# The last twelve convolved tiles woven into the first attention units in a fixed TensorE order, and the slow modulation columns summed once, with none beside top-k

## The chip, the cores and the metric

The kernel runs on one core of one Trainium2 chip. The core has five engines that run their own instruction queues: TensorE (PE; its weight loads are shown apart as PEld), VectorE (DVE), ScalarE (ACT), GpSimd (POOL) and SyncE (SP), which starts the transfers. The metric is the device time of one execution in microseconds, taken as the median of several runs. A profile is one further execution with the hardware profiler on, and its trace gives start and length of every instruction.

## The reference, cut to what matters

One layer of a streaming encoder, for one sequence of 1024 positions with 1024 features, all in float32. It has a mixer sub-layer and a feed-forward sub-layer, both between norms and both modulated by a vector c.

```python
mod = silu(c) @ ada_w + ada_b             # 6 x 1024 values: shift, scale and gate of two sub-layers
h = rmsnorm(x) * (1 + scale) + shift
proj = h @ w_in                           # one projection for everything below
q_lat, kv_lat, k_idx, w_idx, z, xbc, dt, gate_a, gate_b = split(proj)

# A: sparse attention, per block of 128 queries
score = sum_heads(w_idx * relu(q_idx @ k_idx.T))        # only keys of admissible chunks
idx = top_k(score, 256)
logits = q @ kv[idx].T * scale + bias(position)
att = softmax(logits) @ kv[idx] @ w_uv                  # 16 heads, 64 values each

# B: state-space mixer
xbc = silu(causal_depthwise_conv(xbc, width 4) + conv_b)   # 4096 channels
y = ssd(xbc, dt) ; y = rmsnorm(y * silu(z))

out = x + gate * norm((sigmoid(gate_a) * (att @ w_o1) + sigmoid(gate_b) * (y @ w_o2)) @ w_out)
out = out + gate2 * norm(swiglu(modulated norm of out))
```

## The kernel before, in words

Everything is kept transposed: features on the 128 partitions, positions along the free axis in two halves of 512. Each float32 operand of a large product is split into a high part and a low part, and a product is three matmuls (high by high, low by high, high by low). For weights, ScalarE rounds the high part (whi, L151) and GpSimd subtracts it to get the low part (wlo, L152). Raw weight pieces come in 256 KB transfers into four buffers, the high and low parts have three buffers each, so the splits run only a little ahead of TensorE.

The stages in order are: norm and the first 16 columns of the modulation; latents; the scores of the indexer; keys and values; **top-k**, which runs on VectorE and ScalarE as a search with counts and ends in `mark` (L693 to L702) on VectorE, which writes the masks MK; the **attention units**; the rest of the state-space mixer; the merge; the feed-forward layer.

Beside top-k and attention, the kernel runs the **wide column tiles** of the input projection. A wide tile is 128 output features by 1024 positions: 48 matmuls of 128x512 (named pw) into two PSUM banks. There are 56: 32 convolved tiles (`conv`: one ScalarE pass, then three VectorE multiply-adds L904 to L906 that read the PSUM bank, then a silu), 16 z tiles (silu) and 8 a tiles (sigmoid), the latter two through `gate`. The string FILL gives their order: five groups of four convolved tiles, 16 z, 8 a, and three more groups.

An attention unit is one pair of heads (hp, 0 to 7) and one block of 256 queries (u, in U_ORDER 0, 2, 1, 3). `att_scores` makes the queries (puq, 12 matmuls; split into qh on ScalarE and ql on VectorE), adds the bias and the mask on GpSimd (nm, L750), makes the logits (plg), takes their maximum on VectorE while adding nm (L775), and the exponential on ScalarE (L778). `att_out` transposes the probabilities on TensorE (pt, L799), copies them (pc, L802 and L804, by turns on VectorE and ScalarE), multiplies with the values (po, L815) and scales the result (rb). `weave` takes steps of the scores of one unit and the output of the unit before in turn. It can take a third sequence z as well.

The **slow modulation columns** are the 32 of 48 that are needed late. `ada_slow` loads a 128x1024 block in two halves (adaw, two buffers), multiplies each by silu(c) on GpSimd (L316), sums each on VectorE (L317) and adds the two sums on GpSimd (L318). `ada_col` takes the sum over partitions with one TensorE product (adap, L285) and adds the bias on VectorE (mod, L286). `ada_next` starts one column and ends the one three before it.

What sets the order: the program is traced in Python, a scheduler then orders the instructions of each engine by a simulated time, with the traced order as priority. Inside `in_order(engines)` the named engines keep the traced order. Before the change the first 12 attention units (the first three pairs of heads, HP_FIRST) are traced ahead of FILL and their order is left to the scheduler, which puts wide tiles between them; ATT_ORDER is empty, so the later 20 units are left to it as well. PSUM banks come from two pools: `bank_d` has three banks (pw, adap, and pt from the fourth pair of heads on), `bank` five.

Of the kernel before, what the change touches and what calls it, by code (L numbers as in the profile page):

```python
# [17 lines left out]
P = 128  # L18
# [12 lines left out]
LOWEST = -BIGGEST  # L31
QC = 256
ORDERED = (mybir.EngineType.PE, mybir.EngineType.Activation, mybir.EngineType.DVE)
FILL = "xxxxx" + "z" * 16 + "a" * 8 + "xxx"
ADA_FROM = 21
HP_FIRST = 3
LEAD = 1.5
U_ORDER = (0, 2, 1, 3)
ATT_ORDER = ()
NCH = L // QC  # L40
PRODUCT = {n: i for i, n in enumerate("1567342")}
EARLY = 16
# [25 lines left out]
def build(tc, a, dbg=None, stop=99, slots=None):  # L68
# [26 lines left out]
    def half(b):  # L95
        return slice(512 * b, 512 * b + 512)
# [5 lines left out]
    def dump(key, ap, idx=None):  # L102
        if dbg is not None and key in dbg:
            d = dbg[key] if idx is None else dbg[key][idx]
            SP.dma_start(d, ap)
# [203 lines left out]

    def ada_slow(j):  # L310

        acc = EV("adas", (P, 2, P))
        for h in range(2):
            t = wp.tile([P, 4, P], F32, name="adaw", tag="adaw", bufs=2)
            behind(SP.dma_start(t, a["ada_w"][j - 16][:, 4 * h:4 * h + 4]))
            behind(G.tensor_tensor(t, t, cs[:, 4 * h:4 * h + 4, None].to_broadcast([P, 4, P]), op=OP.mult))  # L316
            V.tensor_reduce(acc[:, h], t.rearrange("p k m -> p m k"), axis=AX.X, op=OP.add)  # L317
        G.tensor_tensor(acc[:, 0], acc[:, 0], acc[:, 1], op=OP.add)  # L318
        return j, acc[:, 0]

    AHEAD = 4
    X0 = [[None, None] for _ in range(KT)]
# [522 lines left out]

    att = {}

    def attention(steps, last, beside=lambda: None):

        for s_ in steps + [None] * last:  # L850
            nxt = iter(())
            if s_ is not None:
                hp, u = s_
                if u == U_ORDER[0]:
                    vt = vp.tile([P, NT, P], F32, name="vt", bufs=1)
                    SP.dma_start(vt, d_v[hp])
                    att["w"] = small_weights(a["w_uq"][hp]), vt, load_bias(hp)
                uq, vt, nb = att["w"]
                PR = {}
                nxt = att_scores(u, uq, nb, PR)  # L860
            prev = att.get("prev")
            if prev is None:
                weave(nxt, 5, iter(()), 0)
            else:
                weave(nxt, 5 if s_ else 0, att_out(*prev), 2 * prev[1] + 3, lead=LEAD)
            if s_ is not None:
                att["prev"] = (hp, u, vt, PR)
            beside()

    if stop != 3:  # L870
        attention([(hp, u) for hp in range(HP_FIRST) for u in U_ORDER], 0)
        if stop == 4:
            attention([(hp, u) for hp in range(HP_FIRST, 8) for u in U_ORDER], 1)
    if stop == 4:
        for k in range(KT):
            for b in BS:
                t = EV("attd")
                SP.dma_start(t, d_att[k][:, half(b)])
                dump("attn", t, (k, slice(None), half(b)))
        ctx.close()  # L880
        return


    def wide(c):
        W.plan(col_tile(a["w_in"][c]))
        p = [bank_d("pw") for b in BS]
        dense([(p[b], b, ALL) for b in BS], wpieces(ks8), Hs)
        return p
# [6 lines left out]
            SP.dma_start(dst[:, half(b)], t)  # L895

    def conv(ch, dst):
        p = wide(17 + ch)
        ts = [EV("cv") for b in BS]
        for b in BS:  # L900
            S.activation(ts[b], p[b], AF.Identity, bias=col("conv_b", ch), scale=col("cw3", ch))  # L901
        for s, nm_ in ((1, "cw2"), (2, "cw1"), (3, "cw0")):
            w = col(nm_, ch)
            V.scalar_tensor_tensor(ts[0][:, s:], p[0][:, :512 - s], w, ts[0][:, s:], op0=OP.mult, op1=OP.add)  # L904
            V.scalar_tensor_tensor(ts[1][:, :s], p[0][:, 512 - s:], w, ts[1][:, :s], op0=OP.mult, op1=OP.add)
            V.scalar_tensor_tensor(ts[1][:, s:], p[1][:, :512 - s], w, ts[1][:, s:], op0=OP.mult, op1=OP.add)  # L906
        for b in BS:
            S.activation(ts[b], ts[b], AF.Silu)
            SP.dma_start(dst[:, half(b)], ts[b])
# [8 lines left out]
        if j is not None:  # L918
            late.append(ada_slow(j))

    def conv_group(g, ada):
        for ch, dst in ((16 + g, d_bc[g, 0]), (24 + g, d_bc[g, 1]), (2 * g, d_xs[2 * g]), (2 * g + 1, d_xs[2 * g + 1])):
            conv(ch, dst)
            if ada:
                ada_next()

    n_x, n_z, n_a = iter(range(GROUPS)), iter(range(16)), iter(range(8))
    for i, kind in enumerate(FILL):
        if kind == "x":
            conv_group(next(n_x), i >= ADA_FROM)  # L930
        elif kind == "z":
            t = next(n_z)
            gate(1 + t, d_z[t], AF.Silu)
        elif stop != 3:
            t = next(n_a)
            gate(49 + t, d_sga[t], AF.Sigmoid)
        if kind != "x" and i >= ADA_FROM:
            ada_next()
    if stop != 3:
        with in_order(*ATT_ORDER):  # L940
            attention([(hp, u) for hp in range(HP_FIRST, 8) for u in U_ORDER], 1, ada_next)
    for _ in range(35):
        ada_next()

# [700 lines left out]
```

## Time and profile before

| | us |
|---|---|
| median of 3 runs (lowest, highest) | 2447.46 (2446.3, 2448.2) |
| the profiled execution, its own time | 2449.83 |
| its span, first to last instruction | 2448.1 |
| mean granted TensorE clock | 0.985 |

Of the profile, a row of a timeline has the start and the length in microseconds, the engine, the line, the operation, the tiles out and in, and in brackets the engine's idle time before it with what ended it. A row of the waits has the engine and line that waited, the engine and line waited for, and the total, the number and the longest of the waits. A row of a group has its count, busy time, mean length in nanoseconds, and the idle time ahead. The windows have busy times of the engines in a stretch of time. Names of buffers are those of the program.

### The profile page before, as it was taken

To read this page: it belongs to the slowest core of one execution; us is meant where nothing else is said; L and a number is where in the kernel's file an instruction comes from. 1 tells how busy PE (TensorE), PEld (TensorE's weight loads), DVE (VectorE), ACT (ScalarE), POOL (GpSimd) and SP (SyncE) were. 2 spreads that over 40 slices of the span, in tenths; PEclk is the share of its full clock that TensorE was granted. 3 is DMA by queue.
4 is the path that set the end of the run, shared out by engine and by line. 5 is a ranking of instruction groups with operands and counts; after the bars stand their busy time and mean duration, and the time that the engine had idled before them with its cause. 6 is when DMAs were issued, how large, how long until landed. Compare 5 with 4: busy or idle time off the path is not lost. (4 is left out here: it accounts for less than half of the span.)

```text
span 2448.1 us, 35113 instructions
## 1 busy us (share of the span) xinstructions
PE 2360.6 (96%) x11878; PEld 1915.1 (78%) x11878; DVE 1598.2 (65%) x3109; ACT 1242.6 (51%) x2350; POOL 1052.2 (43%) x854
## 2 busy tenths in 40 slices
PE   7999999999899999999999999999899999999997
PEld 5888888887677787777776777887777888888877
DVE  4466775699765567866457677255466787556776
ACT  3456665577456665555656655353444222335452
POOL 1422112222443334622345445656577555544565
PEclk9999999999999999999999999999999999999999
DMA  7123222523322323311578885465375555328765
GB/s 269 61 88 122 67 70 81 152 93 106 115 90 86 97 93 120 106 40 61 190 226 266 284 261 195 161 213 164 99 241 168 168 191 178 117 95 299 229 212 168
DMA packets 227652, 369.85 MB, mean 151 GB/s; under 512 B 22624, under 2 KB 84752, under 8 KB 227472
## 3 DMA queue, kind: packets, MB, share of 16 engines
q1 hardware_dynamic: 226752, 367.03, 45.9%
q8 instruction: 94, 1.54, 0.3%
q14 instruction: 86, 0.70, 0.1%
q10 hardware_dynamic: 720, 0.58, 0.1%
HBM read 275.74 MB, written 94.92 MB: 151 GB/s over the span
## 5 line engine op out<-in xcount | busy, mean ns | idle before, releaser
L152 POOL TENSOR_TENSOR wlo<-wraw,whi 128x512 fp32r<-128x512 f32 x242 | 330.3, 1367 | 597.7 <-ACT whi L151 536.8
L1254 PE MATMUL p<-xh,wr 128*128 128x512 f32 x880 | 276.2, 392 | 5.8 <-DVE g L1304 4.2
L151 ACT ACTIVATE whi<-wraw 128x512 fp32r<-128x512 f32 x242 | 151.3, 627 | 229.6 <-issue 71.5
L1248 POOL TENSOR_TENSOR wr<-a,wr 128x512 fp32r<-128x512 f32 x110 | 155.6, 1422 | 124.3 <-ACT wr L1247 100.2
L1254 PEld LDWEIGHTS p<-xh,wr 128*128 128x128 f32 x880 | 166.4, 189 | 41.7 <-DVE g L1304 4.6
L1254 PE MATMUL p<-xl,wr 128*128 128x512 f32 x440 | 172.1, 391 | 0.0
L778 ACT ACTIVATE lg<-lg,mx 128x256 f32<-128x256 f32 (+7 forms) x128 | 98.4, 770 | 94.3 <-DVE mx L775 92.2
L1247 ACT ACTIVATE wr<-a 128x512 fp32r<-128x512 f32 x110 | 68.7, 629 | 145.4 <-PE p L1254 118.3
L1254 PE MATMUL p<-h2h,wr 128*128 128x512 f32 x352 | 111.9, 394 | 0.0
L638 ACT ACTIVATE junk<-acc,cand__2182 128x1024 bf16<-128x1024 f32 (+2 forms) x96 | 86.2, 898 | 46.4 <-DVE cand__2182 L681 28.6
L1426 PE MATMUL pfo<-ah,wlo 128*128 128x512 f32 x264 | 103.2, 391 | 2.1 <-POOL wlo L246 2.1
L1426 PE MATMUL pfo<-ah,whi 128*128 128x512 f32 x264 | 103.1, 390 | 0.4 <-ACT whi L245 0.4
L589 DVE SCALAR_TENSOR_TENSOR acc<-rel,widx,acc 128x384 f32<-128x384 f32 (+2 forms) x90 | 87.0, 986 | 24.9 <-ACT rel L584 24.7
L225 PE MATMUL pos<-yh,whi 128*128 128x512 f32 x256 | 100.8, 395 | 2.5 <-ACT yh L1120 2.5
L225 PE MATMUL pos<-yh,wlo 128*128 128x512 f32 x256 | 100.3, 392 | 2.7 <-POOL wlo L152 2.7
L1426 PE MATMUL pfo<-al,whi 128*128 128x512 f32 x264 | 102.7, 389 | 0.0
L799 PE MATMUL pt<-ident,lg 128*128 128x128 f32 x576 | 90.2, 280 | 12.8 <-ACT lg L778 11.2
L584 ACT ACTIVATE rel<-prel 128x512 f32<-128x512 f32 (+3 forms) x160 | 77.1, 523 | 48.5 <-PE prel L583 45.0
L225 PE MATMUL pos<-yw,whi 128*128 128x512 f32 x256 | 99.8, 391 | 0.0
L1254 PEld LDWEIGHTS p<-xl,wr 128*128 128x128 f32 x440 | 83.2, 189 | 17.3
L1515 DVE TENSOR_TENSOR al<-al,ah 128x512 fp32r<-128x512 f32 x66 | 74.6, 1132 | 33.0 <-ACT ah L1510 32.7
L904 DVE SCALAR_TENSOR_TENSOR cv<-pw,vec,cv 128x511 f32<-128x511 f32 (+2 forms) x96 | 71.1, 741 | 34.6 <-ACT cv L901 34.4
(581 smaller groups left out, 7222.6 us busy)
## 6 DMA issues: line engine op xcount, KB each, us to landing
wraw<-w_in SPq DMA_DIRECT2D x130, 256.0 KB, 2.9
a<-w_ffn_in SPq DMA_DIRECT2D x120, 256.0 KB, 3.3
al<-d_a SPq DMA_DIRECT2D x77, 256.0 KB, 4.2
wraw<-w_ffn_out SPq DMA_DIRECT2D x66, 256.0 KB, 3.8
adaw<-ada_w SPq DMA_DIRECT2D x64, 256.0 KB, 2.9
al<-d_ac SPq DMA_DIRECT2D x32, 512.0 KB, 5.5
wraw<-w_o_ssd SPq DMA_DIRECT2D x64, 256.0 KB, 3.1
d_a<-kept SPq DMA_DIRECT2D x33, 256.0 KB, 3.1
```

What stands on the lines that cost most here:

```text
L151: behind(S.activation(hi[:, :kt], raw[:, :kt], AF.Copy))
L152: behind(G.tensor_tensor(lo[:, :kt], raw[:, :kt], f(hi[:, :kt]), op=OP.subtract))
L225: T.matmul(o, wt[:, k0 + i, :], xs[k][xi][b][:, sl], start=pi == 0 and i == 0 and wt is hi and xi == 0, stop=pi == len(pcs) - 1 and i == l ...
L584: S.activation(rel[:, 512 * b:512 * b + w_], pr[:, 0:w_], AF.Relu)
L589: V.scalar_tensor_tensor(acc[i][:, 0:n], rel[:, 0:n], ws, acc[i][:, 0:n], op0=OP.mult, op1=OP.add)
L638: S.activation(jk, y, AF.Sign, scale=-1.0, bias=a_, accum_out=o)
L778: S.activation(lg[:, 0:n], lg[:, 0:n], AF.Exp, scale=-1.0, bias=m, accum_out=mx[:, 3:4])
L799: T.transpose(ptv[:, hh, t, :], PR[hh, t][:, j * P:(j + 1) * P], ident)
L1248: G.tensor_tensor(w[:, 1], src, f(w[:, 0]), op=OP.subtract)
L1254: T.matmul(p, w[:, wi, i], X[x][i][xi], start=start and i == 0 and k == 0, stop=i == 3 and k == 2, skip_group_check=True)
L1426: T.matmul(o, w[wi][:, P * m:P * m + P], x[xi][:, cl], start=j == 0 and k == 0, stop=j == NP - 1 and k == 2)
L1515: V.tensor_tensor(lo, r, f(hi), op=OP.subtract)
```

## The change

Three things are changed. FILL ends after the a tiles, 44 wide tiles, and no column is started beside them. The twelve convolved tiles that are left become a generator, `last_groups`, of 96 steps of six matmuls; the first 12 attention units take it as the third sequence of `weave`, eight steps to a unit, and after each tile `ada_next` is called. TensorE's order is the traced one in that part. The other 20 columns are called beside the 20 later units, where there were 12. And `ada_slow` adds the two products on GpSimd, 128x512, and sums once on VectorE.

```diff
-FILL = "xxxxx" + "z" * 16 + "a" * 8 + "xxx"
-ADA_FROM = 21
+FILL = "xxxxx" + "z" * 16 + "a" * 8
-ATT_ORDER = ()
...
     def ada_slow(j):
 
-        acc = EV("adas", (P, 2, P))
+        ts = []
         for h in range(2):
             t = wp.tile([P, 4, P], F32, name="adaw", tag="adaw", bufs=2)
             behind(SP.dma_start(t, a["ada_w"][j - 16][:, 4 * h:4 * h + 4]))
             behind(G.tensor_tensor(t, t, cs[:, 4 * h:4 * h + 4, None].to_broadcast([P, 4, P]), op=OP.mult))
-            V.tensor_reduce(acc[:, h], t.rearrange("p k m -> p m k"), axis=AX.X, op=OP.add)
-        G.tensor_tensor(acc[:, 0], acc[:, 0], acc[:, 1], op=OP.add)
-        return j, acc[:, 0]
+            ts.append(t)
+        G.tensor_tensor(ts[0], ts[0], ts[1], op=OP.add)
+        acc = EV("adas", (P, P))
+        V.tensor_reduce(acc, ts[0].rearrange("p k m -> p m k"), axis=AX.X, op=OP.add)
+        return j, acc
...
-    def attention(steps, last, beside=lambda: None):
+    def attention(steps, last, beside=lambda: None, z=iter(()), nz=0):
...
-                weave(nxt, 5 if s_ else 0, att_out(*prev), 2 * prev[1] + 3, lead=LEAD)
+                weave(nxt, 5 if s_ else 0, att_out(*prev), 2 * prev[1] + 3, z, nz, lead=LEAD)
...
-    if stop != 3:
-        attention([(hp, u) for hp in range(HP_FIRST) for u in U_ORDER], 0)
...
-    for i, kind in enumerate(FILL):
+    for kind in FILL:
         if kind == "x":
-            conv_group(next(n_x), i >= ADA_FROM)
+            for ch, dst in group(next(n_x)):
+                conv(ch, dst)
...
-        if kind != "x" and i >= ADA_FROM:
-            ada_next()
+
+    def last_groups():
+        for g in n_x:
+            for ch, dst in group(g):
+                W.plan(col_tile(a["w_in"][17 + ch]))
+                w = wpieces(ks8)
+                p = []
+                for b in BS:
+                    p.append(bank_d("pw"))
+                    yield from dense_steps(p[b], b, w, Hs)
+                    yield
+                convolved(ch, dst, p)
+                ada_next()
+
+    woven = last_groups()
     if stop != 3:
-        with in_order(*ATT_ORDER):
-            attention([(hp, u) for hp in range(HP_FIRST, 8) for u in U_ORDER], 1, ada_next)
+        with in_order(mybir.EngineType.PE):
+            attention([(hp, u) for hp in range(HP_FIRST) for u in U_ORDER], 0, z=woven, nz=8)
+            for _ in woven:
+                pass
+        attention([(hp, u) for hp in range(HP_FIRST, 8) for u in U_ORDER], 1, ada_next)
+    for _ in woven:
+        pass
     for _ in range(35):
         ada_next()
```

In the fences below a row has the line, the operation, the tile out and the tiles in, with the running numbers of the tiles, and the shape. The first place is GpSimd beside `mark`. Before, weight splits (wlo) stand behind the adds (adas) and multiplies (adaw) of the modulation columns:

```order
L318 TENSOR_TENSOR adas_7184<-adas_7184 128x128
L316 TENSOR_TENSOR adaw_7266<-adaw_7266,cs_115 128x512
L316 TENSOR_TENSOR adaw_7270<-adaw_7270,cs_115 128x512
L152 TENSOR_TENSOR wlo_7285<-wraw_7283,whi_7284 128x512
L152 TENSOR_TENSOR wlo_7360<-wraw_7358,whi_7359 128x512
L318 TENSOR_TENSOR adas_7265<-adas_7265 128x128
```

After the change, the same engine has weight splits alone up to the first unit, whose masks (nm) and first column come behind them:

```order
L150 TENSOR_TENSOR wlo_5944<-wraw_5942,whi_5943 128x512
L150 TENSOR_TENSOR wlo_5950<-wraw_5948,whi_5949 128x512
L150 TENSOR_TENSOR wlo_6038<-wraw_6036,whi_6037 128x512
L150 TENSOR_TENSOR wlo_6044<-wraw_6042,whi_6043 128x512
L150 TENSOR_TENSOR wlo_6182<-wraw_6180,whi_6181 128x512
L750 TENSOR_TENSOR nm_6061<-nb_6016,dmask_96 128x2x128
L750 TENSOR_TENSOR nm_6099<-nb_6016,dmask_96 128x512
L150 TENSOR_TENSOR wlo_6188<-wraw_6186,whi_6187 128x512
L786 COPY r2_6199<-rr_6035 128x256
L150 TENSOR_TENSOR wlo_6377<-wraw_6375,whi_6376 128x512
L314 TENSOR_TENSOR adaw_6369<-adaw_6369,cs_115 128x512
L750 TENSOR_TENSOR nm_6215<-nb_6016,mk_2179 128x512
```

What moved: the columns no longer stand among the splits that TensorE needs while VectorE marks. Line 152 of before is line 150 of after, and 316 is 314.

The second place is TensorE at the end of top-k. Before, the transposes (pt) and logits (plg) of the first units stand between matmuls of wide tiles (pw):

```order
L225 MATMUL pw_7357<-h3l_445,whi_7359 128x512
L225 MATMUL pw_7357<-h3h_444,wlo_7360 128x512
L225 MATMUL pw_7356<-h7h_651,wlo_7366 128x512
L799 MATMUL pt_2883<-ident_89,lg_2826 128x128
L766 MATMUL plg_2894<-kvth_2015,qh_2875 128x384
L766 MATMUL plg_2894<-kvtl_2016,qh_2875 128x384
L766 MATMUL plg_2894<-kvth_2015,ql_2876 128x384
```

After it, the first unit begins only when the 44th wide tile (pw_5941) is done, with the queries (puq) and the first woven tile (pw_6048):

```order
L223 MATMUL pw_5941<-h7l_657,whi_5949 128x512
L223 MATMUL pw_5941<-h7h_656,wlo_5950 128x512
L223 MATMUL puq_6018<-qnh_779,uh_6011 128x256
...
L233 MATMUL pw_6048<-h3l_440,whi_6037 128x512
L233 MATMUL pw_6048<-h3h_439,wlo_6038 128x512
L766 MATMUL plg_6065<-kvth_2015,qh_6031 128x256
L766 MATMUL plg_6065<-kvtl_2016,qh_6031 128x256
L766 MATMUL plg_6065<-kvth_2015,ql_6032 128x256
L233 MATMUL pw_6048<-h4h_493,whi_6043 128x512
```

What moved: the whole first unit, to behind the wide tiles; before, two units' queries and one's logits were done earlier in top-k.

The third place is TensorE at the border of two units in the woven part. After the change, the values' products (po), the queries and a column's product (adap) are followed by the next tile (pw_7048) and the next transposes in one fixed order:

```order
L815 MATMUL po_6831<-pc_6959,vt_6008 64x128 x2
L223 MATMUL puq_6989<-qnh_808,uh_6756 128x256
...
L223 MATMUL puq_6989<-qnh_813,ul_6757 128x256
L283 MATMUL adap_7024<-ones_92,adas_6373 128x1
L233 MATMUL pw_7048<-h0h_247,whi_7037 128x512
L233 MATMUL pw_7048<-h0l_248,whi_7037 128x512
...
L233 MATMUL pw_7048<-h1h_291,wlo_7038 128x512
L799 MATMUL pt_7058<-ident_89,lg_6854 128x128
L799 MATMUL pt_7058<-ident_89,lg_6899 128x128
```

What moved: a tile now begins right behind the queries of its unit and is spread over it in pieces of six, where the scheduler had spread tiles by its own times.

More of the change, by code (lines that the diff above doesn't have):

```diff
@@ L862, in attention @@
             if prev is None:
-                weave(nxt, 5, iter(()), 0)
+                weave(nxt, 5, iter(()), 0, z, nz)
             else:
-                weave(nxt, 5 if s_ else 0, att_out(*prev), 2 * prev[1] + 3, lead=LEAD)
+                weave(nxt, 5 if s_ else 0, att_out(*prev), 2 * prev[1] + 3, z, nz, lead=LEAD)
             if s_ is not None:
@@ L868, in attention @@
             beside()
-    if stop != 3:
-        attention([(hp, u) for hp in range(HP_FIRST) for u in U_ORDER], 0)
[L872 to L881, printed above, removed]
     def wide(c):
@@ L897, in conv, with convolved @@
     def conv(ch, dst):
-        p = wide(17 + ch)
+        convolved(ch, dst, wide(17 + ch))
+    def convolved(ch, dst, p):
         ts = [EV("cv") for b in BS]
@@ L919, in ada_next, with group @@
             late.append(ada_slow(j))
[L921 to L924, printed above, removed]
-                ada_next()
+    def group(g):
+        return (16 + g, d_bc[g, 0]), (24 + g, d_bc[g, 1]), (2 * g, d_xs[2 * g]), (2 * g + 1, d_xs[2 * g + 1])
     n_x, n_z, n_a = iter(range(GROUPS)), iter(range(16)), iter(range(8))
-    for i, kind in enumerate(FILL):
+    for kind in FILL:
         if kind == "x":
-            conv_group(next(n_x), i >= ADA_FROM)
+            for ch, dst in group(next(n_x)):
+                conv(ch, dst)
         elif kind == "z":
@@ L936, in build @@
             gate(49 + t, d_sga[t], AF.Sigmoid)
-        if kind != "x" and i >= ADA_FROM:
-            ada_next()
-    if stop != 3:
-        with in_order(*ATT_ORDER):
-            attention([(hp, u) for hp in range(HP_FIRST, 8) for u in U_ORDER], 1, ada_next)
+    def last_groups():
[11 more added lines that the diff above has]
+    woven = last_groups()
+    if stop != 3:
+        with in_order(mybir.EngineType.PE):
[5 more added lines that the diff above has]
+        pass
     for _ in range(35):
```

## The prediction

> **What bounds the kernel now.** I read the page's busy times first, then the windows by stage, then the waits of TensorE in each stage, then the engines' timelines around those waits.
>
> ```profile
> PE 2360.6 (96%) x11878; PEld 1915.1 (78%) x11878; DVE 1598.2 (65%) x3109; ACT 1242.6 (51%) x2350; POOL 1052.2 (43%) x854
> core 0: us, PE busy (x) PEld busy (x) DVE busy (x) ACT busy (x) POOL busy (x), PEclk, DMA share, GB/s
> 640.00:690.00 50.00, 40.03 (x162) 31.65 (x161) 47.17 (x72) 12.29 (x23) 23.50 (x18) 0.90 0.34 106
> 690.00:948.00 258.00, 251.45 (x1434) 205.90 (x1433) 151.99 (x450) 157.46 (x259) 96.55 (x102) 0.99 0.29 94
> 948.00:1215.00 267.00, 257.99 (x1701) 197.82 (x1699) 179.53 (x607) 145.61 (x324) 100.65 (x114) 0.99 0.32 99
> ```
>
> TensorE is busy for 96% of the span, so a change that leaves its work alone can only win its idle time and the time it ran at a lower granted clock. The three windows are the stages that the change touches: the end of top-k (640 to 690), the first twelve attention units with the last wide tiles among them (690 to 948), and the twenty later units (948 to 1215). TensorE is idle there for 50 - 40.03 = 9.97, 258 - 251.45 = 6.55 and 267 - 257.99 = 9.01 us. The clock column (0.90, 0.99, 0.99) stands for about 50 x 0.10 = 5.0, 258 x 0.01 = 2.6 and 267 x 0.01 = 2.7 us more. Everything that can be won is 25.5 + 10.3 = 35.8 us. Only the first stage is poor: 15 of its 50 us are lost, against 9.2 of 258 and 11.7 of 267.
>
> ```profile
> PE pw L225 <- POOL wlo L152: 7.0, 2, 4.9
> PE pt L799 <- ACT lg L778: 2.8, 2, 2.5
> ```
> ```profile
> 653.63 0.50 PE L225 MATMUL pw<-h4h,wlo 128*128 128x512 f32 x1 [2.10 <-POOL wlo L152]
> 670.38 0.79 PE L225 MATMUL pw<-h4h,wlo 128*128 128x512 f32 x1 [4.89 <-POOL wlo L152]
> 670.97 0.63 PE L225 MATMUL pw<-h5h,whi 128*128 128x512 f32 x1
> 671.40 0.63 PE L225 MATMUL pw<-h5l,whi 128*128 128x512 f32 x1
> 680.91 0.33 PE L799 MATMUL pt<-ident,lg 128*128 128x128 f32 x1 [2.49 <-ACT lg L778]
> ```
> ```profile
> 646.48 0.46 POOL L318 TENSOR_TENSOR adas<-adas 128x128 f32<-128x128 f32 x1 [5.84 <-DVE mod L286]
> 651.34 4.47 POOL L152 TENSOR_TENSOR wlo<-wraw,whi 128x512 fp32r<-128x512 f32 x2
> 661.72 1.98 POOL L318 TENSOR_TENSOR adas<-adas 128x128 f32<-128x128 f32 x1 [5.92 <-DVE mod L286]
> 668.76 3.05 POOL L152 TENSOR_TENSOR wlo<-wraw,whi 128x512 fp32r<-128x512 f32 x2
> 680.13 0.45 POOL L318 TENSOR_TENSOR adas<-adas 128x128 f32<-128x128 f32 x1 [8.32 <-DVE mod L286]
> ```
> ```profile
> 640.88 1.79 DVE L693 TENSOR_SCALAR acc<-acc,c__2180,sg__2186 128x1024 f32<-128x1024 f32 x3
> 659.60 2.05 DVE L317 TENSOR_REDUCE adas<-adaw 128x128 f32<-128x512 f32 x2
> 661.56 0.14 DVE L286 TENSOR_TENSOR mod<-adap,vec 128x1 f32<-128x1 f32 x1
> 685.35 0.43 DVE L702 TENSOR_SCALAR mk<-run 128x512 bf16<-128x512 f32 x1
> ```
>
> Here is who ends the waits. In the waits of 640 to 690 us, 7.0 us end with GpSimd's low half of a weight tile (wlo, L152); the timeline has them as 2.10 and 4.89 us. But GpSimd is not busy then: each time its 128-wide add of a slow modulation column (L318) has sat 5.84, 5.92 and 8.32 us before it, and the weight halves are queued behind that add. It waits for VectorE, which from 640.88 to 685.78 marks the chosen keys (L693 to L702) and takes the two column sums (2.05 us) only where they fall in that run. So the chain is mark, then column sum, then GpSimd's add, then the weight split, then TensorE. After the 4.89 us the same 512-column matmuls come 0.43 us apart (670.97, 671.40) instead of 0.227 (one wide tile of 48 takes about 11 us, below).
>
> **Part 1: no modulation columns beside top-k.** The new order on GpSimd has weight splits alone there, and one wide tile's pieces are no longer behind anything on VectorE. That removes the 7.0 us. The 2.49 us for an exponential go too: in the order before, the first attention unit's scores stand inside the mark on VectorE; now the first unit starts only after all 44 wide tiles.
>
> ```profile
> 636.83 0.28 PE L285 MATMUL adap<-ones,adas 128*128 128x1 f32 x2
> 647.95 0.28 PE L285 MATMUL adap<-ones,adas 128*128 128x1 f32 x2
> ```
> ```profile
> 739.62 0.28 PE L225 MATMUL puq<-qnh,uh 128*128 128x256 f32 x1
> 739.74 0.28 PE L225 MATMUL puq<-qnl,uh 128*128 128x256 f32 x1
> ```
> ```profile
> 681.20 0.41 DVE L775 CUSTOM_DVE_ANT_0 lg<-plg,nm 128x256 f32<-128x256 f32 x1
> ```
>
> One such pair stands between wide tiles, so a tile takes 647.95 - 636.83 = 11.1 us. By the order before, 40 wide tiles are done at 636.83, and beside them 24 query matmuls and 12 logit matmuls of the first units (0.12 us apart as in the two rows of queries, about 4.6 us with the wider ones) that now come later. Four more tiles end near 636.83 - 4.6 + 4 x 11.1 = 676.6, and the first unit's first need of VectorE (ql, which stands behind the whole mark) comes behind 12 queries and 12 tile matmuls, 12 x 0.12 + 12 x 0.227 = 4.2 us later, near 680.8. The mark without three columns (3 x 2.19 = 6.6 us) and without the first unit's own work (four such logit operations and short ones, 2 us) ends near 677. What is late next is therefore this ql: 3 to 4 us of slack, and a wait of as much as 5 us if the mark does not shorten as I reckon. Bounds for this stage: nothing won, 15.0 won. I take 14, since two of its three stalls have no cause left and the third has slack.
>
> **Part 2: the last twelve tiles woven, TensorE's order fixed.** Work is only moved: the same 576 matmuls. Gone are the stage's own waits, 6.55 idle and about 2.6 of clock, of which the largest looks like this:
>
> ```profile
> 744.89 1.33 PE L799 MATMUL pt<-ident,lg 128*128 128x128 f32 x5 [2.81 <-ACT lg L778]
> 746.44 0.63 PE L225 MATMUL pw<-h0l,whi 128*128 128x512 f32 x1
> 746.87 0.63 PE L225 MATMUL pw<-h0h,wlo 128*128 128x512 f32 x1
> ```
> ```profile
> 740.36 1.28 ACT L908 ACT_TABLE_LOAD   x1
> 742.30 1.28 ACT L778 ACT_TABLE_LOAD   x1
> ```
>
> ScalarE had put a silu of a convolved tile between two exponentials, with a table load before and behind it. In the new order the four exponentials of a unit stand together and a tile's silus come in one place. The fixed order adds its own waits. A woven tile's first matmul now follows a unit's queries at once, and it needs its PSUM bank free: in four of twelve tiles the bank was just used by a modulation column and must be read by VectorE (mod, 0.14 us, above), in the rest by the previous tile's convolution.
>
> ```profile
> L904 DVE SCALAR_TENSOR_TENSOR cv<-pw,vec,cv 128x511 f32<-128x511 f32 (+2 forms) x96 | 71.1, 741 | 34.6 <-ACT cv L901 34.4
> ```
>
> No trace shows the new wait. Its least is nothing (the other engine came first), its most per tile, as long as VectorE is only one instruction behind, is one convolution step and the read, 0.74 + 0.14 = 0.9 us. I take 0.6 for the four and 0.3 for eight, 4.8 us, nearest to the half of a step; twelve at 0.9 would be 11. The stage then changes by 4.8 - 9.2 = -4.4, but some of the old waits (an exponential that is late) will return: I take -3, bounds -9 and +8.
>
> **Part 3: one sum for a column, twelve beside the woven tiles and twenty beside the later units (twelve before).**
>
> ```profile
> L316 POOL TENSOR_TENSOR adaw<-adaw,cs 128x512 f32<-128x512 f32 x24 | 24.9, 1043 | 18.4 <-DMA adaw<-ada_w 16.1 <-DVE adas L317 1.2 <-DVE mx L775 1.1
> L317 DVE TENSOR_REDUCE adas<-adaw 128x128 f32<-128x512 f32 x24 | 25.6, 1067 | 5.9 <-POOL adaw L316 5.9
> L152 POOL TENSOR_TENSOR wlo<-wraw,whi 128x512 fp32r<-128x512 f32 x242 | 330.3, 1367 | 597.7 <-ACT whi L151 536.8
> ```
>
> These are groups of the later units and, last, of the page. A column had two sums on VectorE, 2 x 1.067 = 2.13 us, and a 0.46 us add on GpSimd; it now has one sum, 1.07, and a 128x512 add on GpSimd, which the trace does not show: between 1.04 (the multiply of that size, one tensor operand) and 1.37 (the weight split, two tensors); I take 1.37, the one with two. VectorE is relieved of 32 x 1.07 = 34 us over the kernel, GpSimd gets 32 x 0.91 = 29. In the later units VectorE goes from 12 x 2.13 = 25.6 to 20 x 1.07 = 21.4 and GpSimd from 12 x 2.54 = 30.5 to 20 x 3.45 = 69, out of 267 us of which it was busy 100.65. Both fit, so as busy time the edit costs TensorE nothing; the cover is that GpSimd sits half idle there. What can cost is the place: a column's multiply waits for its transfer, 16.1 us in 24, with the next unit's biased mask (nm, L750) behind it on GpSimd.
>
> ```profile
> PE plg L766 <- DVE mx L775: 3.8, 3, 2.8
> PE pt L799 <- ACT lg L778: 2.4, 3, 1.4
> ```
>
> These two are most of TensorE's 9.01 us of waits there, and VectorE's shorter queue should shorten the first, while eight units that had no column get one. Bounds -9 and +8; I take -2.
>
> **A rule that speaks against part 3.** The rows: a three-element VectorE add, 0.16 us when alone, lasts 1.03 us where GpSimd subtracts weight tiles beside it; it ends at 639.40, about where the first of GpSimd's two operations does.
>
> ```profile
> 634.54 0.16 DVE L648 TENSOR_TENSOR tm__2187<-tm__2187,cand__2182 128x3 f32<-128x3 f32 x1
> 638.10 2.53 POOL L152 TENSOR_TENSOR wlo<-wraw,whi 128x512 fp32r<-128x512 f32 x2
> 638.37 1.03 DVE L645 TENSOR_TENSOR tm__2187<-cnt__2183,kk__2184 128x3 f32<-128x3 f32 x1
> ```
>
> So GpSimd's work holds up VectorE's two-tensor operations, and an add moved from one to the other may be paid on both. [...]
>
> On the clock, the rows have 4.89 us idle followed by slow matmuls, but also 2.81 us idle followed by some (746.44 to 746.87), and 2.10 us followed by none (653.63 lasts 0.50). [...]
>
> **The sum.** The profiled execution took 2449.83 us (span 2448.1). Parts: -14 - 3 - 2 = -19, so about 2431 for such an execution. The median of the three runs is 2447.46, 2.4 us lower, which gives about **2429**.
>
> **Rivals.**
> (1) *The fixed order becomes the wait, and the kernel is slower.* TensorE may not run another tile's matmul while it waits for a bank, a query split or an exponential, as it could where the order followed the scheduler's times. The longest wait for VectorE in the later units, 2.8 us, at each of 12 boundaries is 34 us in place of 9.2: -14 + 24.4 - 2 = +8.4, about 2456. It ends the gain (within 0.2%) from about 1.6 us a unit and makes the kernel slower by over 0.2% from about 2.4. Against it: TensorE's only long waits in before's stage are three for an exponential (6.0 us in all), and six matmuls lie between neighbouring steps of a unit, 1.4 us of cover.
> (2) *Only the first stage wins.* GpSimd's adds hold VectorE (the rule above), or columns ahead of the masks delay twenty units by some 0.4 us each: the later units go from -2 to +6, and the sum is -14 - 3 + 6 = -11: about 2437. The same comes out if the mark does not shorten: 5 us of wait for ql and 2.6 of clock, as behind the 4.89 us.
> (3) *The stall moves with the columns and the change removes nothing.* On GpSimd the columns stand among weight splits again, now those of the woven tiles. If a column's add waits for VectorE there as it did beside the mark, the 7.0 us and the lost clock of the first stage come back: +15, about 2444 to 2447. For it: the order of GpSimd in the woven units. Against it: VectorE is busy 151.99 of 258 us there, 47.17 of 50 beside the mark, so nothing on it lasts 6 us.
> (4) *Everything is won*: -33, about 2415.
>
> **How the numbers follow.** The forecast has 0.57, (1) 0.15, (2) 0.18, (3) 0.07, (4) 0.03. A measurement of this kernel can tell about 0.2% from no change, which is 4.9 us: faster is below 2442.6, slower above 2452.4. Faster collects the forecast, (4), most of (2) and a little of (1), 0.77; same (3) and pieces of (1) and (2), 0.13; slower two thirds of (1), 0.10. The range takes in (2), (3) and the bounds of parts 1 to 3 together (about 2416 with nearly all won): 2416 to 2449; outside lie most of (1) and (4).
>
> **What would show it.** Right: from the marked keys to the first unit, TensorE has no wait for wlo above 1 us and a granted clock near 1.00; VectorE's mark is one run without column sums; the sum's group has 32 instead of 64; waits in the woven units are below 1 us and name VectorE's mod or convolution. Wrong: a wait of several us for ql at the first unit (3), a wait at each woven unit (1), VectorE operations of 1 us that were 0.2 beside the new add, or longer waits for mx in the later units (2). The weakest steps are the 4.8 us for the fixed order and the later units' -2, both worked out from operations of another kind.

## The result and the profile after

The changed kernel takes 2431.81 us (median of 4 runs, 2430.83 to 2433.8) beside 2446.88 us for the kernel before on the same chip: a ratio of 0.9941, with a 95% interval of 0.9924 to 0.9959. In another group of runs (6 runs) it took 2431.43 beside 2448.52, a ratio of 0.9926 (0.9913 to 0.9939). That is 15 to 17 us less; 2429 us was forecast. The profiled execution took 2432.21 us, its span is 2430.3 us, and the granted clock is 0.991 where it was 0.985.

First the busy line of the page, then the three stages in windows (span of the window, busy time of TensorE, weight loads, VectorE, ScalarE and GpSimd, granted clock, DMA share, GB/s), all of the changed kernel:

```profile
PE 2352.2 (97%) x11878; PEld 1909.0 (79%) x11878; DVE 1572.8 (65%) x3077; ACT 1226.1 (50%) x2336; POOL 1074.3 (44%) x854
```
```profile
640.00:690.00 50.00, 50.00 (x239) 42.06 (x238) 37.27 (x53) 14.97 (x29) 17.34 (x12) 1.00 0.26 90
690.00:948.00 258.00, 248.68 (x1468) 203.78 (x1466) 158.44 (x484) 148.83 (x258) 114.36 (x110) 1.00 0.29 97
948.00:1215.00 267.00, 260.78 (x1716) 199.48 (x1716) 172.44 (x580) 148.14 (x335) 126.19 (x127) 1.00 0.37 119
```

The end of top-k has no idle time left, where 9.97 us were idle, and its clock is 1.00 instead of 0.90: 15 us, all that could be had there. From 690 to 948 the idle time is 9.32 instead of 6.55, and the clock column is 1.00 instead of 0.99, so that stage is about even. From 948 to 1215 it is 6.22 instead of 9.01, again at 1.00 instead of 0.99: some 5.5 us. The clock column has two digits, so the shares of the clock in the two long windows are good to about 1.3 us each (0.005 of the window). The windows have fixed ends while the work moves forward, so the sum is better read at one point of the program, the first matmul of the attention's output projection, in the rows of that matmul before and after (count, shortest, median and longest in ns, first and last start):

```profile
L235 PE MATMUL poa<-ath,whi x128: 387/389/792, 1321.5 to 1476.2; 128*128 128x512 f32 x128
```
```profile
L233 PE MATMUL poa<-ath,whi x128: 387/389/632, 1298.7 to 1456.0; 128*128 128x512 f32 x128
```

It starts at 1298.7 instead of 1321.5, 22.8 us earlier. Two windows that end there say what went, first of before, then of after:

```profile
640.00:1321.50 681.50, 652.37 (x3859) 515.18 (x3857) 436.73 (x1221) 379.80 (x749) 263.60 (x267) 0.98 0.37 117
```
```profile
640.00:1298.70 658.70, 641.48 (x3870) 508.89 (x3869) 417.97 (x1192) 363.13 (x736) 293.53 (x274) 1.00 0.37 121
```

Idle time went from 29.13 to 17.22, 11.9 us less; busy time, in which the lower clock is hidden, from 652.37 to 641.48, 10.9 less. Of the 11.9 us, 10.0 lie in the three windows. The other 1.9 are a wait at the projection's own start, for ScalarE's ath, which is 3.6 us long before and 1.7 after; no part of the prediction reckoned with it. Of the 22.8 us the span keeps 17.8. The rest is lost behind the point: that stretch lasts 2448.1 - 1321.5 = 1126.6 us before and 1131.6 after. The same kernel run again starts this matmul at 1301.5 in a span of 2430.0, so there the stretch lasts 1128.5; over the profiles of all the runs below it lasts 1126.3 to 1132.7. The 5 us are thus no more than the scatter of single profiles.

### The profile page after: what moved, and what is told of

Its sections match the earlier page's. It is cut to its first block, busy times and chain, and to the rows that moved or that the text cites. A ratio compares the mean times of both kernels' runs of the same rounds, so it can differ in the third digit from the quotient of the medians.

```text
span 2430.3 us, 35062 instructions
## 1 busy us (share of the span) xinstructions
PE 2352.2 (97%) x11878; PEld 1909.0 (79%) x11878; DVE 1572.8 (65%) x3077; ACT 1226.1 (50%) x2336; POOL 1074.3 (44%) x854
## 5 line engine op out<-in xcount | busy, mean ns | idle before, releaser
L314 POOL TENSOR_TENSOR adaw<-adaw,cs 128x512 f32<-128x512 f32 x64 | 66.3, 1041 | 90.5 <-DMA adaw<-ada_w 78.5
```

## The experiments

Each kernel was timed in five rounds beside the kernel before, in three groups, each on one chip. Ratios are to the kernel before; the last column is the start of the first projection matmul in its profile, with before at 1321.5. These starts carry scatter from the head of the program: the first matmul of the first wide tile stands between 71.0 and 74.3 us in these profiles, at 73.0 in before.

| kernel | median us | ratio, 95% interval | projection starts |
|---|---|---|---|
| cols_late | 2445.87 | 0.9989 (0.9978 to 1.0001) | 1314.8 |
| one_sum | 2450.32 | 1.0007 (0.9998 to 1.0017) | 1321.4 |
| woven_alone | 2448.15 | 0.9995 (0.9984 to 1.0006) | 1316.3 |
| no_order | 2424.27 | 0.9901 (0.9882 to 0.9921) | 1293.2 |
| two_sums | 2442.75 | 0.9976 (0.9965 to 0.9987) | 1310.6 |
| units_late | 2437.27 | 0.9955 (0.9940 to 0.9970) | 1307.9 |
| cols_other_bank | 2421.84 | 0.9892 (0.9875 to 0.9909) | 1290.0 |
| free_other_bank | 2424.49 | 0.9907 (0.9889 to 0.9926) | 1294.0 |
| after_again | 2431.43 | 0.9926 (0.9913 to 0.9939) | 1301.5 |
| other_bank_again | 2419.87 | 0.9877 (0.9862 to 0.9892) | 1291.7 |
| cols_doubled | 2416.05 | 0.9864 (0.9850 to 0.9877) | 1284.8 |
| sum_twice | 2432.55 | 0.9935 (0.9922 to 0.9948) | 1299.9 |

### One part at a time

**cols_late**: the kernel before, with the columns moved away from top-k and nothing else.

```diff
-ADA_FROM = 21
+ADA_FROM = 29
```

> The kernel before with one number changed: no slow column beside the eight a tiles and the top-k, twelve beside the last twelve tiles and twenty beside the later units, as in the change; still two sums a column, no weaving, no fixed order. My theory (the 15 us lost from 640 to 690 us come from columns whose sums stand in VectorE's mark, with GpSimd's weight splits behind them): TensorE's waits for wlo in that stage go from 7.0 us to under 1, the mark is one run of about 36 us, and 9 to 14 of the 15 us are won, less 0 to 4 for eight more columns in the later units: 2433 to 2440 us. Rival (the weaving wins the time, because the first unit no longer stands in the mark): the wlo waits stay or are replaced by waits of the first unit, and the time is within 4 us of before.

The theory is half right, and its time is not: what came is what the rival expected. The waits for wlo are gone, but the stage still loses 6.23 us of idle time and 3.5 of clock. The window, and TensorE's, VectorE's and ScalarE's timelines at the place:

```profile
640.00:690.00 50.00, 43.77 (x206) 36.03 (x205) 39.14 (x81) 21.43 (x38) 13.02 (x11) 0.93 0.20 67
```
```profile
668.95 0.47 PE L799 MATMUL pt<-ident,lg 128*128 128x128 f32 x1 [6.23 <-ACT lg L778]
```
```profile
638.42 1.79 DVE L693 TENSOR_SCALAR acc<-acc,c__2180,sg__2186 128x1024 f32<-128x1024 f32 x3
...
668.11 0.26 DVE L775 CUSTOM_DVE_ANT_0 lg<-plg,nm 128x128 f32<-128x128 f32 x1
```
```profile
668.41 0.40 ACT L778 ACTIVATE lg<-lg,mx 128x128 f32<-128x128 f32 x1 [9.07 <-DVE mx L775]
```

The first unit's transposes wait for an exponential, this waits for the maximum (L775), and the maximum stands behind 30 us of marking on VectorE. Before, TensorE met that same queue at the weight splits; with the splits free it reaches the first unit sooner and meets it there. The gain is 2.7 us, which cannot be told from none. The rival laid this on the missing weaving; units_late, below, shows that the first unit's place is enough.

**one_sum**: the kernel before with the new `ada_slow` alone.

```diff
-            V.tensor_reduce(acc[:, h], t.rearrange("p k m -> p m k"), axis=AX.X, op=OP.add)
-        G.tensor_tensor(acc[:, 0], acc[:, 0], acc[:, 1], op=OP.add)
+            ts.append(t)
+        G.tensor_tensor(ts[0], ts[0], ts[1], op=OP.add)
+        V.tensor_reduce(acc, ts[0].rearrange("p k m -> p m k"), axis=AX.X, op=OP.add)
```

> The kernel before with the new form of a column alone: one add of 128x512 on GpSimd, one sum on VectorE. My theory: GpSimd's add no longer waits for VectorE, but a column's two buffers stay taken until the sum, which still stands in the mark, so the next column's transfer and multiply, and the splits behind them, still wait: the wlo waits of 640 to 690 us fall from 7.0 to 2 to 6, VectorE has 32 x 1.07 us less, and the time is 3 to 9 us less than before (2438 to 2444). Rival A (the load of VectorE is what counts): the mark and the later units shorten and the time falls by 10 or more. Rival B (GpSimd's larger adds block VectorE): no change or slower.

No gain at all, against the 3 to 9 us of the theory. Beside top-k the wait has only changed its name: the waits of TensorE from 640 to 690 us, and GpSimd's timeline.

```profile
PE pw L225 <- POOL wlo L152: 7.3, 1, 7.3
```
```profile
665.44 1.04 POOL L316 TENSOR_TENSOR adaw<-adaw,cs 128x512 f32<-128x512 f32 x1 [6.43 <-DMA adaw<-ada_w]
...
672.67 3.45 POOL L152 TENSOR_TENSOR wlo<-wraw,whi 128x512 fp32r<-128x512 f32 x2
```

GpSimd no longer waits for VectorE's sums but for transfers. The one that ends at 665.44 was issued at 662.81, when VectorE's sum, still in the mark (661.72 to 662.77), had given a buffer back; the next was issued at 668.04, behind GpSimd's own add, which gives back the second buffer. The splits are behind them as before. VectorE's 34 us less of work over the kernel, with GpSimd's larger adds against them, buy nothing measurable.

**woven_alone**: the changed kernel with the old column and with columns beside the a tiles.

```diff
             gate(49 + t, d_sga[t], AF.Sigmoid)
+            ada_next()
```

(The old `ada_slow` is put back as well.)

> The changed kernel with the old column (two sums) and with columns beside the eight a tiles again: weaving and fixed order alone. My theory: the wlo waits beside the mark come back (5 to 10 us with the lost clock), and the first unit may wait for the mark as well; the woven stage wins about nothing; 2440 to 2450 us. Rival (weaving wins the time): 2430 to 2436 us.

As the theory had it. The waits of 640 to 690 us, then those of 690 to 948 us that concern a tile's start:

```profile
PE pw L223 <- POOL wlo L150: 6.4, 2, 3.3
```
```profile
PE pw L233 <- DVE mod L284: 8.6, 6, 1.9
```

So none of the three parts of the change can be told from nothing when it stands alone.

### Parts together

**two_sums** is the changed kernel with the old `ada_slow` (the diff of one_sum turned round); **units_late** is two_sums without weaving and without a fixed order, with the first unit still traced behind the 44 wide tiles:

```diff
-        with in_order(mybir.EngineType.PE):
-            attention([(hp, u) for hp in range(HP_FIRST) for u in U_ORDER], 0, z=woven, nz=8)
+        with in_order():
+            attention([(hp, u) for hp in range(HP_FIRST) for u in U_ORDER], 0)
```

> Two sums, columns late as in the change, the first unit traced behind the 44 wide tiles, but the last twelve tiles traced behind the twelve units (no weaving, no fixed order): only the place of the first unit, added to cols_late. My theory: the 6.2 us wait for an exponential at the first unit and its clock go, as the mark is over by then, and the gain is near that of the two parts together: 2430 to 2438 us. Rival (the weaving itself is needed): TensorE waits at the first units or later as it did, 2442 us or more.

> The changed kernel with the old column (two sums on VectorE, a 128-wide add on GpSimd): what the one sum is worth once the rest is in place. My theory now (two things had to go together beside top-k: the columns out of the mark and the first unit behind it; the one sum is a small relief of VectorE in the woven and the later units): the stage from 640 to 690 us stays without waits, waits for mod, mx and the copies grow by 2 to 6 us, 2434 to 2441 us. Rival A (the one sum is worth nothing): 2430 to 2433. Rival B (it carries the gain): 2442 or more.

units_late, 0.9955, gains 11 us: to move the columns away and the first unit behind the mark is a gain where the columns alone gave none that can be told (cols_late), and it needs no weaving. From 640 to 690 us it has TensorE busy for all 50 us, like the changed kernel. With the weaving and its fixed order on top, two_sums, it is 0.9976, so these two cost some 5 us there (on one chip; the intervals overlap by 0.0005). Against the change (0.9941, and 0.9926 again), two_sums is 9 to 12 us slower, above the theory's range. The one sum, worthless alone, is worth that once the rest is in place.

The last statement went against the theory in size, and **sum_twice** asks why: the changed kernel with its one sum issued twice.

```diff
         V.tensor_reduce(acc, ts[0].rearrange("p k m -> p m k"), axis=AX.X, op=OP.add)
+        V.tensor_reduce(acc, ts[0].rearrange("p k m -> p m k"), axis=AX.X, op=OP.add)
```

> The changed kernel with its one sum issued twice, so VectorE has the load of two sums (1.07 us a column more) while the order on GpSimd and the buffers' turns stay. My theory (two_sums lost its 9 us through VectorE's load in the later units): units 1 to 12 end within 2 us of the change, the last unit 6 to 12 us later, 2438 to 2444 us. Rival (what counts is that GpSimd no longer waits for VectorE's sums before the next column): within 3 us of the change.

The rival holds: 2432.55 us beside 2431.43 for the change on the same chip. The windows of the later units, first of two_sums, then of sum_twice:

```profile
948.00:1215.00 267.00, 255.48 (x1670) 193.05 (x1669) 179.68 (x585) 142.65 (x322) 110.03 (x124) 1.00 0.33 109
```
```profile
948.00:1215.00 267.00, 259.35 (x1706) 199.98 (x1703) 186.28 (x594) 148.02 (x333) 127.46 (x128) 1.00 0.37 119
```

sum_twice has more work on VectorE (186.28 against 179.68 us) and leaves TensorE less idle (7.65 against 11.52). So the load of VectorE is not what the old column cost. What differs first is GpSimd's queue. Its waits from 934 to 1075 us, of two_sums and of sum_twice:

```profile
POOL adas L316 <- DVE rr L777: 23.0, 6, 5.6
POOL adaw L314 <- DMA adaw<-ada_w: 17.6, 17, 2.1
POOL adas L316 <- PE pt L797: 10.4, 2, 5.2
POOL r L784 <- DVE rr L777: 6.3, 3, 3.1
POOL adas L316 <- DVE adas L315: 5.6, 4, 2.2
POOL adas L316 <- DVE mod L284: 0.8, 1, 0.8
```
```profile
POOL adaw L314 <- DMA adaw<-ada_w: 32.4, 20, 2.9
POOL r L787 <- DVE rr L780: 10.6, 6, 2.4
```

With two sums GpSimd's small add (adas, L316 in that kernel) stands still for 39.8 us in 13 places, waiting for sums on VectorE that wait for other work in turn. With one sum GpSimd adds its own two products and never asks VectorE. It stands longer for transfers instead (32.4 us for 17.6), so that all its waits in this stretch add up to 64.5 us in two_sums and 49.7 in sum_twice. The last of the 32 units is scaled (rb) at 1156.2 us in two_sums, at 1145.9 in sum_twice and at 1146.5 in the change, while the twelfth is at 933.3, 934.0 and 933.5: the old column costs nothing in the woven units and about 10 us in the later ones. That GpSimd's standstill is the cause is what is left, and it is not shown. By which of the units' own steps it reaches TensorE is not settled: TensorE's waits from 948 to 1215 us in two_sums are spread over six causes, none over 3.5 us in total. And the scheduler orders the later units by itself, so that TensorE's order differs between these kernels from some 930 to 945 us on; no run holds that order still.

### The fixed order

**no_order** is the changed kernel with the woven units left to the scheduler:

```diff
-        with in_order(mybir.EngineType.PE):
+        with in_order():
             attention([(hp, u) for hp in range(HP_FIRST) for u in U_ORDER], 0, z=woven, nz=8)
```

> The changed kernel without the fixed order of TensorE (the woven tiles are traced in the same place, the scheduler orders them). My theory: the fixed order as such is worth little, since it pays 4.6 us of waits for VectorE's mod and saves waits for exponentials of like size: 2428 to 2438 us, with fewer waits for mod and more for lg. Rival (the order is what keeps the exponentials in time): the waits for lg return to 6 us or more with 2 to 3 us of clock, 2438 us or more.

It is faster than the change, 0.9901 (0.9882 to 0.9921) against 0.9941 (0.9924 to 0.9959); against the change's second timing, 0.9926 (0.9913 to 0.9939), the intervals overlap a little. It is faster than either side had expected. The waits of TensorE from 690 to 948 us, first in the change, then in no_order:

```profile
PE pw L233 <- DVE mod L284: 4.6, 4, 1.3
PE plg L766 <- DVE mx L775: 1.6, 1, 1.6
PE pt L799 <- ACT pc L804: 1.6, 1, 1.6
PE pt L799 <- ACT lg L778: 0.9, 1, 0.9
PE pw L233 <- DVE cv L893: 0.4, 2, 0.2
```
```profile
PE plg L766 <- DVE mx L775: 1.7, 1, 1.7
PE pt L799 <- ACT lg L778: 1.1, 1, 1.1
PE plg L766 <- ACT pc L804: 0.8, 1, 0.8
PE pt L799 <- ACT pc L804: 0.2, 1, 0.2
```

The waits for exponentials (6.0 us in this stage of before) stay away without the fixed order as well, so it is not the order that removed them. Nor need it be the weaving: units_late, which does not weave, has 1.4 us of them here and cols_late, which leaves units and tiles where they were, 0.8. But there other waits stand in their place, and TensorE is idle for 7.0 and 6.9 us in this stage, against 4.0 in no_order. What removed these waits stays open. What the fixed order added is the waits for mod. In TensorE's timeline of the change they are the starts of four woven tiles, two of which are shown, with VectorE's rows ahead of the first:

```profile
751.49 0.50 PE L233 MATMUL pw<-h0h,whi 128*128 128x512 f32 x1 [0.99 <-DVE mod L284]
...
792.68 0.50 PE L233 MATMUL pw<-h0h,whi 128*128 128x512 f32 x1 [1.30 <-DVE mod L284]
```
```profile
750.29 0.42 DVE L819 TENSOR_TENSOR rb<-po,rb 128x256 f32<-128x256 f32 x1
750.62 0.74 DVE L892 SCALAR_TENSOR_TENSOR cv<-pw,vec,cv 128x509 f32<-128x509 f32 x1
751.28 0.15 DVE L284 TENSOR_TENSOR mod<-adap,vec 128x1 f32<-128x1 f32 x1
```

The column's product is issued at 750.21, and VectorE reads it only behind two other instructions.

**cols_other_bank** takes their cause away: the column's product goes to the pool of five banks. **free_other_bank** does it without the fixed order.

```diff
     def ada_col(j, acc):
-        p = bank_d("adap")
+        p = bank("adap")
```

> The changed kernel with a column's one-column product in the pool of five PSUM banks instead of the three that the wide tiles use: no woven tile waits for VectorE's mod. My theory: the 4.6 us of waits for mod go and the time falls by 3 to 5 us, to 2426 to 2429. Rival (such a wait only moves: the tile then waits for the convolution before it, or a logit for the bank): within 1.5 us of the change, 2430 to 2433.

> No fixed order and the column's product in the other pool, both against the change. My theory (without the fixed order the waits for mod are gone already, no_order had none): within 2 us of no_order, 2422 to 2427. Rival (the two gains are separate): 2418 to 2421.

In cols_other_bank the waits for mod are gone and the gain is larger than they were: 2421.84 us, below the 2426 of the theory. To tell whether that was the chip, the change and cols_other_bank were run side by side.

> The changed kernel once more, beside the two below on one chip. 2430 to 2436 us.

> The column's product in the other pool once more (4.6 us of waits for mod were removed, and the run before showed 10 us less than the change on another chip). My theory: the waits are worth their 4.6 us and what they pushed behind them, 5 to 11 us less than the change on this chip. Rival (the difference was between chips): under 4 us less.

On one chip the other bank takes 2419.87 us and the change 2431.43, 11.6 us apart (5 to 11 were expected), with intervals that do not meet (0.9862 to 0.9892, 0.9913 to 0.9939). At the projection's start it is 9.8 us ahead. Of these, 2.7 are there at the first matmul of the first wide tile (71.6 for 74.3 us), where the two kernels do not differ yet: scatter. From that matmul on, TensorE's order is the same in both up to about 920 us, and the change needs 845.8 us for that stretch where the other bank needs 840.2. The first profiles of the same two kernels, after and cols_other_bank, say 845.7 and 840.2. So the bank is worth 5.5 us in the woven units, 4.9 of them idle time of TensorE. The remaining 1.6 us come later, where the order differs, and have no cause here. free_other_bank (0.9907) is not told apart from no_order (0.9901): without the fixed order there was no wait for mod to remove. From the first wide tile to the projection the three (cols_other_bank, no_order and free_other_bank) need 1219.0, 1219.9 and 1222.4 us, the change 1226.8. These runs do not rank them; that the first is ahead of the change is shown, that the other two are is likely.

**cols_doubled** puts two columns beside each woven tile, on top of the other bank:

```diff
                 convolved(ch, dst, p)
                 ada_next()
+                ada_next()
```

> The column's product in the other pool, and two columns beside each woven tile (24) instead of one, so 8 beside the later units instead of 20. My theory: columns cost nothing in the woven units (units end at the same time with one sum and with two) and cost in the later ones, where GpSimd's masks and VectorE's maxima are close to the path; the later units lose their waits for mx, 3 to 8 us less than the column in the other pool alone. Rival (the woven units have no room: GpSimd has the weight splits there as well): waits for wlo or mx in the woven units, and no gain or a loss.

The windows of the woven and the later units in cols_doubled:

```profile
690.00:948.00 258.00, 253.76 (x1526) 208.96 (x1524) 173.04 (x526) 149.91 (x265) 154.18 (x145) 1.00 0.37 122
948.00:1215.00 267.00, 265.42 (x1736) 205.69 (x1734) 165.05 (x555) 153.45 (x347) 93.08 (x95) 1.00 0.33 107
```

The woven units carry 24 columns without a new wait of TensorE over 0.3 us, and the later ones are down to 1.58 us of idle time. 2416.05 us is the fastest of all twelve kernels and 15.4 us ahead of the change. Against the other bank alone (2419.87) the intervals overlap, so the 3.8 us between these two are likely and not shown; the projection starts 6.9 us earlier.

## Why the prediction was right, point by point

**Part 1, -14.** Measured: 9.97 us of idle time and 5.0 of clock are gone, -15. The chain was as described, and the marks came out close. The rows of the change, VectorE and TensorE:

```profile
636.87 2.77 DVE L693 TENSOR_SCALAR acc<-acc,c__2180,sg__2186 128x1024 f32<-128x1024 f32 x3
...
671.45 1.40 DVE L702 TENSOR_SCALAR mk<-run 128x512 bf16<-128x512 f32 x1
677.00 0.69 DVE L738 SCALAR_TENSOR_TENSOR ql<-puq,qh 128x512 fp32r<-128x512 f32 x1 [4.15 <-ACT qh L737]
```
```profile
674.67 0.28 PE L223 MATMUL puq<-qnh,uh 128*128 128x256 f32 x1
```

The first unit starts at 674.67 (676.6 reckoned). The mark lasts 36.0 us without columns and ends at 672.85 (677 reckoned). It began 4 us sooner: before, three columns' sums stood among the counts of top-k as well (605.0 to 632.1 us), though 1.1 us of the 4 is there at the first wide tile already. So ql finds VectorE idle for 4.15 us. But the heading named one cause and there were two. The prediction let the wait for the exponential go because the unit starts later, and that was needed: cols_late shows that without it nearly the whole gain of the columns turns into a 6.23 us wait of the first unit. The 14 us belong to the columns and the unit's new place together, and units_late shows that these two are enough for it.

**Part 2, -3.** The stage came out about even (9.32 idle at full clock against 6.55 and 2.6 of clock). The fixed order's own waits were put at 4.8 us and are 4.6 for mod and 0.4 for the convolution, in four and two places. That this total came out is luck: the four were counted right, but each is longer than taken (1.0 to 1.3 us for 0.6), and the eight convolution waits are nearly none (0.4 for 2.4). The step of 0.9 at most held for a VectorE that is one instruction behind, and at all four it was two behind (a scaling rb and a convolution step, or two convolution steps). The term that was too small is that of the old waits that return: 1.4 us taken, 4.1 measured (mx 1.6, pc 1.6, lg 0.9). So the sign "below 1 us and name mod or convolution" failed. What the prediction also did not see is that the exponentials come in time without the fixed order. With the column's product in the wide tiles' banks the order is likely a loss: no_order is 6 to 10 us faster by the ratios. With the product in the other pool it is none that can be told (cols_other_bank and free_other_bank).

**Part 3, -2.** The later units won 2.8 us of idle time and about 2.7 of clock, -5.5. The size was off for a reason that the working missed: it priced the one sum by busy times (34 us off VectorE, 29 us onto GpSimd, both under cover). sum_twice shows that the busy time on VectorE is worth nothing that can be told here, and two_sums that the form of the column is worth 9 to 12 us. The waits of GpSimd for VectorE that it ends are the likely way, which is argued and not shown. The group of the new add and of the sum in the change:

```profile
L316 POOL TENSOR_TENSOR adaw<-adaw x32: 1262/1288/1301, 78.3 to 1072.4; 128x512 f32<-128x512 f32 x32
L318 DVE TENSOR_REDUCE adas<-adaw x32: 1042/1065/1095, 688.5 to 1073.7; 128x128 f32<-128x512 f32 x32
```

The add takes 1.29 us, between the bounds of 1.04 and 1.37, and the 32 adds and 32 sums all keep their length (1.30 and 1.10 us at most).

**The sum** of -19 was -22.8 at the projection's start and -17.8 in the span. The parts were -15, about 0 and -5.5, so parts 2 and 3 were off by some 3 us each in opposite directions: that the sum came this near is in part luck, while the main term, part 1, came by its mechanism.

**The rivals.** (1), the slower one, needed 1.6 us of waits a unit to end the gain (its own sum gives nearer 1.7); they are 9.3 us in the stage, under 0.8 a unit. But its direction was right, as cols_other_bank shows. (2) did not come: waits for mx in the later units are 4.2 us, 3.8 before, 0.4 more where the rival needed 8. Of its two causes, no run shows GpSimd's adds holding VectorE: the adds kept their length (1.30 us at most), and of the 122 VectorE operations that ran beside one of them from 690 us on, none is over 0.03 us longer than the shortest of its form. All of these read a PSUM tile (plg, pw, pt, puq, po or adap) or one tensor at most. An operation like that of the prediction's row, with two tensors and neither of them a PSUM tile, did not run beside an add, so that what an add does to it was not shown. (3) did not come in the change, but a stall did move in two of its parts: in cols_late to the first unit, in one_sum to a transfer. The change escapes because it moves both the columns and the first unit. (4) did not come: 15.5 us of idle time are left in the two later stages. On the clock, no wait from 640 us to the projection is longer than 1.7 us in the change, and the granted clock of that stretch is 1.00.

## What to carry to other kernels

Where a chain of queues feeds TensorE, freeing one link can show the next one that hangs on the same engine, as the 7.0 us of waits for weight splits became one of 6.23 us at the first unit in cols_late: three edits that each measured as nothing gave 15 us together, so undo parts from the whole as well as adding them to the start. An operation that goes from one engine to a second and back to the first should be priced by the waits it plants in the first engine's queue too, not by its busy time alone: here VectorE's busy time was worth nothing that could be told, though that the 39.8 us of such waits on GpSimd are what cost was not shown. And before an order is fixed by hand, ask which shared buffer each instruction follows: a one-column product in the wide tiles' banks cost four waits of about 1 us, and another pool was one word away.

## What the runs showed that was not expected

VectorE operations with one tensor input can also last longer beside one of GpSimd's weight splits. Two marks (mk) of the change do, 1.78 us for 0.68 and 1.40 for 0.43; the rows are GpSimd's and VectorE's of the change, then VectorE's of before, with no split beside it:

```profile
648.21 1.55 POOL L150 TENSOR_TENSOR wlo<-wraw,whi 128x512 fp32r<-128x512 f32 x1 [2.68 <-ACT whi L149]
648.53 1.78 DVE L702 TENSOR_SCALAR mk<-run 128x1024 bf16<-128x1024 f32 x1
669.97 2.60 POOL L150 TENSOR_TENSOR wlo<-wraw,whi 128x512 fp32r<-128x512 f32 x1 [3.68 <-ACT whi L149]
```
```profile
656.14 0.68 DVE L702 TENSOR_SCALAR mk<-run 128x1024 bf16<-128x1024 f32 x1
```

The first mark is that of 1.78 us, where before has 0.68. The last, at 671.45 beside the second split, lasts 1.40 us, where the same operation took 0.43 before (at 685.35). The second split is long too, 2.60 us where one alone, at 675.40, takes 1.29; but VectorE runs two operations with two tensor inputs in that time as well (at 669.67 and 670.74), so this cannot be laid on the mark. None of it reached TensorE, which was busy throughout.
